# Order-only edges in the queues of ScalarE and VectorE, and a combination in two parts, in a decoder layer of split fp32r products

## The chip, the cores and the metric

The kernel runs on one core of a Trainium2 chip. The metric is the device time of one execution in microseconds (us). Times are compared as medians of several executions; the profile and the trace come from one further execution, whose own time stands beside its span.

## The reference, cut to what matters

One layer of a decoder over 256 tokens of width 2048, batch 1, in float32: a gated FFN half-step, a mixing stage (differential attention and an mLSTM scan from one input projection, one output projection), a second gated FFN half-step, and a last norm.

```python
x = x + 0.5 * swiglu(rmsnorm(x, ffn1_norm), ffn1_w_gate, ffn1_w_up, ffn1_w_down)   # D_FF = 5632
h = rmsnorm(x, mix_norm)
a_q, a_k, a_v, m_q, m_k, m_v, m_o, m_i, m_f = split(h @ w_in)
y_a = diff_attention(...)          # 4 heads, causal
y_b = mlstm(...) * sigmoid(m_o)    # 4 heads, causal
x = x + concat(y_a, y_b) @ w_out
x = x + 0.5 * swiglu(rmsnorm(x, ffn2_norm), ffn2_w_gate, ffn2_w_up, ffn2_w_down)
return rmsnorm(x, final_norm)
```

Nearly all of the work is products of a 256-row activation with weight matrices that are read once from HBM.

## The kernel before, in words

**Products in two halves.** Every operand of a large product is split in two fp32r parts: `hi`, a copy of it in fp32r on ScalarE (line 116), and `lo`, the rest, a subtraction on VectorE (line 117). For each pair of tiles `mms` (lines 142 to 149) issues three matmuls of 128x512: hi of the activation with hi of the weights (line 146), lo with hi (line 147), and, after all jobs of the call, hi with lo (line 149). So line 149 is the first to need a VectorE result (`wl`), line 146 the first to need ScalarE's (`wh`). Split weights live in `wsp`, four buffers of each half; a buffer comes free when the matmuls that read it are done.

**Pairs of outputs by seven products.** Two neighbouring chunks of 512 output columns are computed together by class `Paired` (lines 359 to 500), a Strassen-like scheme on the first `ns` blocks of the contraction (`ns` is 4 in the gate and up products, 2 in the first pair of them, 3 or 1 in the down products, 3 in the input projection, 2 in the output projection). `first` works on four PSUM banks p1, p6, p7, p5: for each block j, `load(j)` (line 381) fetches four 128x512 weight tiles into one `raw` buffer (pool `wr`, four buffers) by two DMAs on SyncE's queue, then VectorE forms two pair sums into `sums[j]` (line 388; the tile takes a slot of pool `wrp`, five slots, tag `rawp`, which the plain loads use too) and a third sum in place (line 390). `p57(j)` splits the sums and multiplies into p7 and p5; `p16(j)` splits two tiles of `raw`, multiplies into p1 and p6, and then has POOL issue a DMA that adds one tile of `raw` to another (line 409). For the last block p16 comes before p57. `combine` (lines 430 to 439) then joins the banks: ScalarE copies p1 to `u` (434), VectorE adds p6 to it (435) and it to p7 (436), ScalarE copies p7 to `u3` (437), VectorE subtracts (438, 439). `second` goes on in p1, p7 and p5 with the blocks' remaining tiles (`bare`, `upper`) and with `plain` units, ordinary products of the rest of the contraction, each loaded as one 512 KB `rawp` tile. `third` finishes the other output chunk and is left as a stream of units.

**The order of the work.** `Chain.run` (lines 511 to 527) writes the program order by hand: it steps through `first` of the next pair and lets units of the last pair's `third` run in between, then calls `combine`, then the end of the last pair (gate product, transposes, additions), then `second`. TensorE's own queue follows this order. The queues of the other engines are laid out by the framework's scheduler when the program is built, by priorities: loads, sums and splits are placed as if they stood 400 instructions earlier (`AHEAD`, with `high_priority`), and "seam" work, which is what stands between two pairs (the combination, the gate's SiLU at line 325, its product at line 329, the halved copy `part` at line 292), 440 earlier (`soon`). Each engine then runs its queue strictly in the order laid out. Semaphores between engines are made by the framework.

**The FFNs.** `ffn` (lines 535 to 584) runs 11 chunks of the hidden width in parts of 3, 3, 3 and 2; each part ends with two pairs of the down product. In the last part these pairs have one block (`ns == 1`) and three plain units. In the first FFN the first gate product is an ordinary one (`linear`, line 562), during which `load_xt` (line 591) loads and splits the transposed input; `sum_xt` (line 618) makes the sums of one activation block: two scalings on ScalarE (through line 344), three additions on VectorE (283 to 285) and a split. It is called once in `load_xt` and again at line 567, and two more times from the list `pending`.

## Time and profile before

| | |
|---|---|
| median of 3 runs | 1796.76 us (1793.56 to 1799.55) |
| the profiled execution | 1798.07 us |
| its span | 1796.4 us |
| granted TensorE clock, mean over the span | 0.997 |
| instructions | 23431 |
| read from HBM / written | 349.56 MB / 2.10 MB |

The span runs from the first to the last instruction of the program. In the timelines a row is: start in us from the span's start, duration in us, engine, line, operation, tile written and tiles read, shapes, number of instructions merged in the row, and in brackets the idle time of the engine before it with what ended it. PE is TensorE's matmuls, PEld its weight loads, DVE VectorE, ACT ScalarE, POOL GpSimd, SP SyncE.

### The profile page before, as it was taken

To read this page: it belongs to the slowest core of one execution; us is meant where nothing else is said; L and a number is where in the kernel's file an instruction comes from. 1 tells how busy PE (TensorE), PEld (TensorE's weight loads), DVE (VectorE), ACT (ScalarE), POOL (GpSimd) and SP (SyncE) were. 2 spreads that over 40 slices of the span, in tenths; PEclk is the share of its full clock that TensorE was granted. 3 is DMA by queue.
4 is the path that set the end of the run, shared out by engine and by line. 5 is a ranking of instruction groups with operands and counts; after the bars stand their busy time and mean duration, and the time that the engine had idled before them with its cause. 6 is when DMAs were issued, how large, how long until landed. Compare 5 with 4: busy or idle time off the path is not lost.

```text
span 1796.4 us, 23431 instructions
## 1 busy us (share of the span) xinstructions
PE 1773.1 (99%) x8033; PEld 1463.6 (81%) x8033; DVE 1566.1 (87%) x1895; ACT 1163.8 (65%) x1512; POOL 176.7 (10%) x220
## 2 busy tenths in 40 slices
PE   9999999999999999999999999999999999999998
PEld 6788888887888878987888888888888888888886
DVE  6988899988998877796787988999899988998886
ACT  6666666666666656676566766666666666666664
POOL 0001100111002100000000000001100111002100
PEclk9999999999999999999999999999999999999999
DMA  9777877887788863665656665778877788778864
GB/s 340 220 226 223 239 230 231 258 237 223 218 261 235 257 236 122 209 215 196 196 191 197 192 194 165 220 240 249 233 243 232 249 236 243 211 254 239 262 193 152
DMA packets 124649, 402.76 MB, mean 224 GB/s; under 512 B 14001, under 2 KB 14513, under 8 KB 124273
## 3 DMA queue, kind: packets, MB, share of 16 engines
q1 hardware_dynamic: 96192, 349.35, 56.6%
q0 software_dynamic: 27328, 49.82, 16.5%
q10 hardware_dynamic: 1008, 2.09, 0.3%
q8 instruction: 63, 1.03, 0.2%
q14 instruction: 58, 0.47, 0.1%
HBM read 349.56 MB, written 2.10 MB: 196 GB/s over the span
## 4 chain that ended last, share of the span: by engine, by line
PE 86%; DMA 5%; issue 4%; DVE 4%; ACT 1%; SPq 0%; POOL 0%; DVEq 0%; POOLq 0%; ACTq 0%
PE acc L146 28%; PE acc L149 27%; PE acc L147 27%; DVE wl L117 2%; DMA raw<-in_wu_dram 2%; DMA rawp<-in_wu_dram 2%; PE tr L307 1%; ACT wh L116 1%; DVE sums L388 1%; DMA raw<-raw 0%; PE tr L250 0%; PE sc L946 0%; SPq L173 0%; PE num L897 0%; PE tr L689 0%
## 5 line engine op out<-in xcount | busy, mean ns | idle before, releaser
L116 ACT CAST wh<-raw 128x1024 fp32r<-128x1024 f32 (+3 forms) x448 | 402.0, 906 | 282.6 <-PE acc L147 180.4
L146 PE MATMUL acc<-wh,xt 128*128 128x512 f32 (+3 forms) x1444 | 559.8, 389 | 3.1 <-ACT wh L116 3.0
L147 PE MATMUL acc<-wh,xt 128*128 128x512 f32 (+3 forms) x1444 | 557.0, 387 | 0.0
L117 DVE TENSOR_TENSOR wl<-raw,wh 128x1024 fp32r<-128x1024 f32 (+3 forms) x448 | 459.7, 1039 | 86.2 <-ACT wh L116 83.2
L116 ACT CAST wh<-rawp 128x1024 fp32r<-128x1024 f32 (+1 forms) x358 | 372.7, 1044 | 156.0 <-PE acc L147 133.3
L117 DVE TENSOR_TENSOR wl<-rawp,wh 128x1024 fp32r<-128x1024 f32 (+1 forms) x358 | 430.9, 1207 | 44.9 <-ACT wh L116 41.6
L146 PE MATMUL acc<-wh,xs 128*128 128x512 f32 (+2 forms) x1071 | 420.2, 393 | 6.7 <-ACT wh L116 2.9
L147 PE MATMUL acc<-wh,xs 128*128 128x512 f32 (+2 forms) x1071 | 414.8, 388 | 0.0
L149 PE MATMUL acc<-wl,xt 128*128 128x512 f32 (+3 forms) x1444 | 398.5, 386 | 0.4 <-DVE wl L117 0.4
L149 PE MATMUL acc<-wl,xs 128*128 128x512 f32 (+2 forms) x1071 | 335.9, 389 | 2.7 <-DVE wl L117 2.5
L146 PEld LDWEIGHTS acc<-wh,xt 128*128 128x128 f32 x1444 | 271.5, 188 | 60.6 <-ACT wh L116 5.8
L147 PEld LDWEIGHTS acc<-wh,xt 128*128 128x128 f32 x1444 | 271.6, 188 | 54.0
L149 PEld LDWEIGHTS acc<-wl,xt 128*128 128x128 f32 x1444 | 269.7, 188 | 54.7 <-DVE wl L117 0.8
L146 PEld LDWEIGHTS acc<-wh,xs 128*128 128x128 f32 x1071 | 201.5, 188 | 49.0 <-ACT wh L116 3.7
L149 PEld LDWEIGHTS acc<-wl,xs 128*128 128x128 f32 x1071 | 200.1, 188 | 47.3 <-DVE wl L117 6.9
L409 POOL DMA_DIRECT2D raw<-raw x141 | 121.5, 863 | 1187.8 <-DVE wl L117 852.4
L147 PEld LDWEIGHTS acc<-wh,xs 128*128 128x128 f32 x1071 | 201.5, 188 | 39.4 <-DVE xs L112 0.4
L388 DVE TENSOR_TENSOR sums<-raw 128x1024 f32<-128x1024 f32 x141 | 171.8, 1219 | 43.7 <-DMA raw<-in_wu_dram 38.9
L116 ACT CAST wh<-sums 128x1024 fp32r<-128x1024 f32 x141 | 148.5, 1053 | 83.7 <-PE acc L147 62.6
L117 DVE TENSOR_TENSOR wl<-sums,wh 128x1024 fp32r<-128x1024 f32 x141 | 171.8, 1219 | 12.5 <-ACT wh L116 10.1
L390 DVE TENSOR_TENSOR raw<-sums,raw 128x512 f32<-128x512 f32 x141 | 96.3, 683 | 0.8
L293 POOL DMA_DIRECT2D xres<-part x48 | 44.4, 1002 | 265.6 <-ACT part L292 264.4
(199 smaller groups left out, 804.4 us busy)
## 6 DMA issues: line engine op xcount, KB each, us to landing
rawp<-in_wd_dram SPq DMA_DIRECT2D x96, 512.0 KB, 5.6
rawp<-in_wu_dram SPq DMA_DIRECT2D x94, 512.0 KB, 7.5
raw<-in_wg_dram SPq DMA_DIRECT2D x89, 512.0 KB, 7.1
rawp<-in_wg_dram SPq DMA_DIRECT2D x86, 512.0 KB, 6.0
raw<-in_wu_dram SPq DMA_DIRECT2D x82, 512.0 KB, 7.8
raw<-in_wd_dram SPq DMA_DIRECT2D x80, 512.0 KB, 6.2
raw<-raw POOLq DMA_DIRECT2D x141, 256.0 KB, 6.2
rawp<-in_win_dram SPq DMA_DIRECT2D x50, 512.0 KB, 4.9
```

The source lines that it names most:

```text
L116: nc.scalar.copy(hi, src)
L117: nc.vector.tensor_tensor(out=lo, in0=src, in1=hi.bitcast(F32), op=ALU.subtract)
L146: nc.tensor.matmul(acc, lh, rh, start=first, stop=False, skip_group_check=on)
L147: nc.tensor.matmul(acc, ll, rh, start=False, stop=False, skip_group_check=on)
L149: nc.tensor.matmul(acc, lh, rl, start=False, stop=last, skip_group_check=on)
L293: nc.gpsimd.dma_start(xres[:, hb, c * CW:(c + 1) * CW], t, accum_op=ALU.add)
L307: nc.tensor.transpose(tr[:, i, hb * P:(hb + 1) * P], hs[hb][:, k * P:(k + 1) * P], ident)
L388: nc.vector.tensor_tensor(out=sums[j], in0=raw[:, 0:4:3, :], in1=raw[:, 2:3, :].to_broadcast([P, 2, CW]), op=ALU.add)
L390: nc.vector.tensor_tensor(out=raw[:, 2, :], in0=sums[j][:, 0, :], in1=raw[:, 3, :], op=ALU.add)
L409: nc.gpsimd.dma_start(raw[:, 2, :], raw[:, 1, :], accum_op=ALU.add)
```

## The change

It adds edges between two instructions of the same engine that fix their order in its queue and bring no semaphore (dependency class NoSync), and moves some steps in program order:

- Weight splits are counted (`splits`). A pair sum (line 388) may not stand ahead of the low half of the fourth split before it (`SUMS = 4`).
- Seam instructions are put in a list with the count at that time (`ahead_of_splits`); the split that is made four or more splits later (`SLACK = 4`) must stand behind them: its hi behind those of ScalarE, its lo behind those of VectorE. These are `part`, the gate's SiLU and product, and four of the six steps of the combination.
- The combination is cut in two: `combine` (copy of p1, addition of p6) is called right behind the last block's p16, `combine_rest` behind its p57, both inside `first`; before, all of it was called behind the units of the other stream.
- In pairs with one block, `second` puts the first plain unit ahead of `bare` and `upper`, and the hi split of `bare` must stand behind the second copy (`u3`).
- The second call of `sum_xt` moves from line 567, which stands behind four units of the first up product, into `load_xt`, where it now stands beside the first call at the last two units (6 and 7) of the first gate product.

```diff
@@ -43,6 +43,8 @@
 WARM = 10
 LAST_UNITS = 3
 CUTS = ((0, 544, 0), (1088, 1568, 1), (544, 1088, 0), (1568, 2048, 1))
+SLACK = 4
+SUMS = 4
 FLUSH = 3
 
 G_FFN1, G_MIX, G_FFN2, G_CW, G_CB, G_ATT, G_ML = 0, 16, 32, 48, 80, 88, 96
@@ -113,8 +115,29 @@
                                        op0=ALU.mult, op1=ALU.subtract)
 
     def split(src, hi, lo):
-        nc.scalar.copy(hi, src)
-        nc.vector.tensor_tensor(out=lo, in0=src, in1=hi.bitcast(F32), op=ALU.subtract)
+        return (nc.scalar.copy(hi, src),
+                nc.vector.tensor_tensor(out=lo, in0=src, in1=hi.bitcast(F32), op=ALU.subtract))
+
+
+
+    splits, queued = [], ([], [])
+
+    def after(late, early):
+
+        tc.add_manual_dep(late.ins, early.ins.name,
+                          mybir.DependencyInfo(mybir.DependencyClass.NoSync, mybir.DependencyReason.DATA),
+                          reason="order")
+
+    def ahead_of_splits(i, ins):
+        queued[i].append((len(splits), ins))
+
+    def split_weights(src, hi, lo):
+        made = split(src, hi, lo)
+        for late, q in zip(made, queued):
+            while q and len(splits) >= q[0][0] + SLACK:
+                after(late, q.pop(0)[1])
+        return made
+
 
     def pair_tiles(pool, tag, shape):
         return (pool.tile(shape, F32R, tag=tag + "h", name=nm(tag + "h")),
@@ -135,8 +158,9 @@
         with tc.high_priority(offset=AHEAD):
             o = 0
             for n in pieces:
-                split(raw[:, o:o + n, :], hi[:, o:o + n, :], lo[:, o:o + n, :])
+                made = split_weights(raw[:, o:o + n, :], hi[:, o:o + n, :], lo[:, o:o + n, :])
                 o += n
+        splits.append(made)
         return hi, lo
 
     def mms(jobs):
@@ -289,7 +313,7 @@
 
         t = wk("part")
         with soon():
-            nc.scalar.activation(t, acc, AF.Copy, scale=0.5)
+            ahead_of_splits(0, nc.scalar.activation(t, acc, AF.Copy, scale=0.5))
         nc.gpsimd.dma_start(xres[:, hb, c * CW:(c + 1) * CW], t, accum_op=ALU.add)
 
     def residual(accs, c, scale, parts):
@@ -322,11 +346,11 @@
     def gate(src, r):
         s = wk("sg")
         with soon():
-            nc.scalar.activation(s, src, AF.Silu, scale=r)
+            ahead_of_splits(0, nc.scalar.activation(s, src, AF.Silu, scale=r))
         return s
 
     def gated(src, r, s):
-        nc.vector.scalar_tensor_tensor(s, src, r, s, op0=ALU.mult, op1=ALU.mult)
+        ahead_of_splits(1, nc.vector.scalar_tensor_tensor(s, src, r, s, op0=ALU.mult, op1=ALU.mult))
         return s
 
     def soon(extra=40):
@@ -385,14 +409,16 @@
                     for i, w in enumerate((self.wa, self.wb)):
                         load_pair(raw[:, 2 * i:2 * i + 2, :], w, self.k0 + 2 * j)
                     sums[j] = wrp.tile([P, 2, CW], F32, tag="rawp", name=nm("sums"))
-                    nc.vector.tensor_tensor(out=sums[j], in0=raw[:, 0:4:3, :],
-                                            in1=raw[:, 2:3, :].to_broadcast([P, 2, CW]), op=ALU.add)
+                    made = nc.vector.tensor_tensor(out=sums[j], in0=raw[:, 0:4:3, :],
+                                                   in1=raw[:, 2:3, :].to_broadcast([P, 2, CW]), op=ALU.add)
+                    if len(splits) >= SUMS:
+                        after(made, splits[-SUMS][1])
                     nc.vector.tensor_tensor(out=raw[:, 2, :], in0=sums[j][:, 0, :], in1=raw[:, 3, :], op=ALU.add)
 
             def halves_of(src):
                 with tc.high_priority(offset=AHEAD):
                     t = pair_tiles(wsp, "w", [P, 2, CW])
-                    split(src, *t)
+                    splits.append(split_weights(src, *t))
                 return t
 
             def p57(j):
@@ -412,15 +438,20 @@
             p57(0)
             yield
             p16(0)
+            if last == 0:
+                self.combine()
             for j in range(1, self.ns):
                 load(j)
                 if j < last:
                     p57(j)
                 p16(j)
+                if j == last:
+                    self.combine()
                 if j % 2 and j < last - 1 or j == last:
                     yield
                 if j == last:
                     p57(j)
+            self.combine_rest()
             yield
 
         def steps(self):
@@ -428,13 +459,19 @@
             return {1: 2, 2: 3, 3: 3}.get(self.ns, 4)
 
         def combine(self):
-            u, u3 = wk("u"), wk("u3")
-            p1, p5, p6, p7 = self.p1, self.p5, self.p6, self.p7
+
+            self.u = wk("u")
             with soon():
-                nc.scalar.copy(u, p1)
-                nc.vector.tensor_tensor(out=u, in0=p6, in1=u, op=ALU.add)
-                nc.vector.tensor_tensor(out=p7, in0=p7, in1=u, op=ALU.add)
-                nc.scalar.copy(u3, p7)
+                ahead_of_splits(0, nc.scalar.copy(self.u, self.p1))
+                ahead_of_splits(1, nc.vector.tensor_tensor(out=self.u, in0=self.p6, in1=self.u, op=ALU.add))
+
+        def combine_rest(self):
+            u, u3 = self.u, wk("u3")
+            p5, p6, p7 = self.p5, self.p6, self.p7
+            with soon():
+                ahead_of_splits(1, nc.vector.tensor_tensor(out=p7, in0=p7, in1=u, op=ALU.add))
+                self.copied = nc.scalar.copy(u3, p7)
+                ahead_of_splits(0, self.copied)
                 nc.vector.tensor_tensor(out=p6, in0=p5, in1=u3, op=ALU.subtract)
                 nc.vector.tensor_tensor(out=p5, in0=p5, in1=u, op=ALU.subtract)
 
@@ -456,7 +493,9 @@
             def bare(j):
                 with tc.high_priority(offset=AHEAD):
                     t = pair_tiles(wsp, "w", [P, 2, CW])
-                    split(self.raws[j][:, 1:3, :], *t)
+                    splits.append(split_weights(self.raws[j][:, 1:3, :], *t))
+                    if self.ns == 1:
+                        after(splits[-1][0], self.copied)
                 mms([self.job(n11, j, A2, t, 0, False, False, True), self.job(n21, j, B2, t, 1, False, False, True)])
 
             def upper(j0):
@@ -464,20 +503,28 @@
                     t = pair_tiles(wsp, "w", [P, 2, CW])
                     js = range(j0, min(j0 + 2, self.ns))
                     for i, j in enumerate(js):
-                        split(self.raws[j][:, 3, :], t[0][:, i, :], t[1][:, i, :])
+                        made = split_weights(self.raws[j][:, 3, :], t[0][:, i, :], t[1][:, i, :])
+                splits.append(made)
                 mms([self.job(n12, j, S4, t, i, False, False, True) for i, j in enumerate(js)])
 
             for i in range(max(self.ns, len(self.rest))):
                 aside(side)
-                if i < self.ns:
-                    bare(i)
-                    if i % 2 or i == self.ns - 1:
-                        upper(i - i % 2)
+                def blocks():
+                    if i < self.ns:
+                        bare(i)
+                        if i % 2 or i == self.ns - 1:
+                            upper(i - i % 2)
+
+                if self.ns > 1:
+                    blocks()
                 if i < len(self.rest):
                     if i < len(self.rest) - 1:
                         self.plain(self.wa, self.rest[i], (n11, n21))
                     else:
                         self.plain(self.wa, self.rest[i], (n11, n21), True)()
+                if self.ns == 1:
+
+                    blocks()
                 flush(0 if i % 2 else None)
                 aside(mid)
             return [n11, n21]
@@ -521,7 +568,6 @@
                     done += 1
                 flush(1)
                 aside(side)
-            p.combine()
             self.end()
             half(p.second())
             self.put(p.third(last_units), len(p.rest), lambda: end(p.accs()))
@@ -564,7 +610,6 @@
                     stream = units(au, xp, wu[0], KD, fine=True)
                     for _ in range(KD // UK - NP):
                         next(stream)
-                    first[1]()
                     chain.put(stream, NP, functools.partial(end, au))
                 else:
                     np_ = NP
@@ -607,7 +652,7 @@
                 hi, lo = plain_pair(xp1, u)
             for t in range(UK):
                 split_gain(raw[:, t, :], G_FFN1 + k + t, hi[:, t, :], lo[:, t, :])
-        if u == KD // UK - 1:
+        if u >= KD // UK - NP_FIRST:
             sum_xt()
         if u >= KD // UK - NT:
```

## Rows read from the trace of the kernel before

**Rows 1.** The page, part 1: busy us of each engine, share of the span, instructions.
```profile
PE 1773.1 (99%) x8033; PEld 1463.6 (81%) x8033; DVE 1566.1 (87%) x1895; ACT 1163.8 (65%) x1512; POOL 176.7 (10%) x220
```

**Rows 2.** Busy time by stretch: length, engines, granted clock, DMA share, GB/s.
```profile
14.00:667.00 653.00, 647.95 (x2886) 533.77 (x2885) 578.03 (x647) 422.02 (x506) 71.61 (x82) 1.00 0.80 242
667.00:677.00 10.00, 6.98 (x23) 4.95 (x22) 9.27 (x12) 4.85 (x7) 0.00 (x0) 0.83 0.58 179
677.00:1786.00 1109.00, 1106.63 (x5099) 918.65 (x5098) 969.18 (x1213) 725.35 (x981) 101.68 (x123) 1.00 0.70 214
```

**Rows 3.** Waits of TensorE's matmuls: us in total, times, longest.
```profile
PE acc L146 <- ACT wh L116: 5.9, 7, 2.5
PE acc L149 <- DVE wl L117: 2.9, 7, 0.6
...
PE acc L146 <- ACT u L434: 0.4, 1, 0.4
```

**Rows 4.** Timeline of TensorE, 199 to 209 us.
```profile
200.19 0.39 PE L147 MATMUL acc<-wh,xs 128*128 128x512 f32 x1
201.17 0.73 PE L149 MATMUL acc<-wl,xs 128*128 128x512 f32 x2 [0.59 <-DVE wl L117]
...
208.10 0.61 PE L149 MATMUL acc<-wl,xs 128*128 128x512 f32 x2
```

**Rows 5.** Timeline of VectorE, 186 to 209 us.
```profile
190.74 1.23 DVE L388 TENSOR_TENSOR sums<-raw 128x1024 f32<-128x1024 f32 x1 [3.06 <-DMA raw<-in_wu_dram]
...
198.77 1.21 DVE L388 TENSOR_TENSOR sums<-raw 128x1024 f32<-128x1024 f32 x1
199.90 1.21 DVE L117 TENSOR_TENSOR wl<-raw,wh 128x1024 fp32r<-128x1024 f32 x1
...
206.37 1.23 DVE L117 TENSOR_TENSOR wl<-raw,wh 128x1024 fp32r<-128x1024 f32 x1 [1.24 <-ACT wh L116]
```

**Rows 6.** Timeline of VectorE, pieces from 82 to 1738 us.
```profile
82.63 2.35 DVE L388 TENSOR_TENSOR sums<-raw 128x1024 f32<-128x1024 f32 x2
...
140.84 1.23 DVE L388 TENSOR_TENSOR sums<-raw 128x1024 f32<-128x1024 f32 x1
...
152.30 1.22 DVE L117 TENSOR_TENSOR wl<-rawp,wh 128x1024 fp32r<-128x1024 f32 x1
...
161.68 1.22 DVE L117 TENSOR_TENSOR wl<-sums,wh 128x1024 fp32r<-128x1024 f32 x1
...
1736.90 1.22 DVE L388 TENSOR_TENSOR sums<-raw 128x1024 f32<-128x1024 f32 x1
```

**Rows 7.** Timeline of TensorE, 661 to 677 us.
```profile
661.58 0.62 PE L149 MATMUL acc<-wl,xs 128*128 128x512 f32 x2
...
667.70 0.39 PE L147 MATMUL acc<-wh,xs 128*128 128x512 f32 x1
669.93 0.50 PE L146 MATMUL acc<-wh,xs 128*128 128x512 f32 x1 [1.85 <-ACT u L437]
670.27 0.40 PE L147 MATMUL acc<-wh,xs 128*128 128x512 f32 x1
670.51 0.63 PE L149 MATMUL acc<-wl,xs 128*128 128x512 f32 x2
672.30 0.67 PE L146 MATMUL acc<-wh,xs 128*128 128x512 f32 x1 [1.17 <-DVE acc L439]
...
676.05 0.39 PE L146 MATMUL acc<-wh,xt 128*128 128x512 f32 x1
```

**Rows 8.** Timeline of ScalarE, 655 to 674 us.
```profile
665.01 1.57 ACT L116 CAST wh<-raw 128x1024 fp32r<-128x1024 f32 x2 [6.71 <-PE acc L149]
666.49 0.58 ACT L434 COPY u<-acc 128x512 f32<-128x512 f32 x1
```

**Rows 9.** One operation of the combination: duration ns min/median/max, first and last start.
```profile
L436 DVE TENSOR_TENSOR acc<-acc,u x44: 687/691/700, 56.8 to 1767.0; 128x512 f32<-128x512 f32 x44
```

**Rows 10.** Timeline of ScalarE, 33 to 46 us.
```profile
39.24 1.27 ACT L325 ACTIVATE sg<-acc,rstd 128x512 f32<-128x512 f32 x2 [1.95 <-POOL rstd L231]
40.40 1.70 ACT L344 ACTIVATE xg<-xraw,prm 128x256 f32<-128x256 f32 x4
```

## The prediction

> **What bounds the kernel now.** I read the busy shares first [rows 1]: TensorE's matmuls cover 1773.1 of 1796.4 us, so only time in which TensorE starts nothing can be won. Then the busy time by stretch [rows 2]: from 677 to 1786 us the weight loads are busy 918.65 of 1109 us (0.828) at granted clock 1.00; from 14 to 667 us 533.77 of 653 (0.817); from 667 to 677 us only 4.95 of 10, at clock 0.83. So the losses sit in the first FFN and above all in ten microseconds at its end. Then TensorE's waits [rows 3] for what ended them. Last the timelines around single waits, matmuls beside the two queues that feed them.
>
> One measure is needed throughout. A matmul record lasts 0.39 us, but the next one starts after 0.227 us: in [rows 4] the pair that starts at 208.10 lasts 0.61, so its second starts 0.22 after its first. An idle time in the list of waits is therefore short by 0.39 - 0.227 = 0.16 us: between 200.19 and 201.17 pass 0.98 us, 0.75 more than the pace, where the row says 0.59.
>
> The Trainium skill ("Perfetto Trace Analysis", Identifying the Most-Contended Engine) calls matmul occupancy a bad measure of headroom and the busy share of the weight loads a good one. By it, at 0.828 everywhere, re-ordering could give 653 - 533.77/0.828 = 8.4 us and 10 - 4.95/0.828 = 4.0 us, 12.4 in all; by matmul occupancy it would be 653 - 647.95 + 10 - 6.98 = 8.1. The waits below, counted from start to start, bear out the larger one.
>
> **Part 1, pair sums held back.** VectorE takes its queue in order. At 190.74 a pair sum heads it and waits 3.06 us for a load [rows 5]; the queue then runs without a gap until past 203. At 198.77 the sum of the pair's last block goes first and takes 1.13 us until the next start, and the low half that starts at 199.90 is the one TensorE waits for at 201.17 [rows 4, 5]. That sum belongs to the block whose low half starts at 206.37, four splits on. The new edge puts each sum behind the low half of the fourth split before it: here behind the one at 199.90, which then starts 1.13 us sooner. The wait costs 0.75, so it goes. I counted the same way, in the order of VectorE's queue: 80 of the 141 sums (the first at 82.63, the last at 1736.90 [rows 6]) stand ahead of the low half that they must now follow, and each wait of TensorE for a low half in the list has such a sum right in front of it. The list has 2.9 us in 7 waits [rows 3]; with 0.16 each, 2.9 + 7 x 0.163 = 4.0 us. All are shorter than 1.13 us.
>
> What is late next: at 206.37 + 1.23 = 207.60 a low half is ready whose matmul starts at 208.10 [rows 4, 5], so 0.50 of margin meets 0.75 regained, and 0.25 is lost again. I take 3.8 us, with 0 and 4.5 (two shorter waits that the list leaves out) as ends.
>
> What it costs: no instruction is added, each edge joins two instructions of one engine and asks for no semaphore (class NoSync). Twelve sums now run nine splits ahead: the one at 140.84 moves behind the low half at 152.30 [rows 6], 11.5 us later, still three splits before its own at 161.68. Its 1.13 us moves out of a stretch with margin into the next. It hides in the idle time before the sum at 190.74 (3.06 us) and its like. Without that cover it is 1.13 us on the low halves behind it. I take 0. The sum frees no slot of the loads (those of `raw` go with the last split of the block), so SyncE's queue is not held up by it; it takes its own `rawp` slot later, which frees that slot for a load. POOL's accumulating transfer follows the block's first split and stays behind it.
>
> **Part 2, the combination in two parts, and seam work ahead of later splits.** At 666 us is the pair with one block (`ns == 1`). Its last p1 product starts at 661.58 [rows 7], so the copy of p1 could run from about 662.2. ScalarE waits 6.71 us for a free split buffer, splits two tiles for work after the seam at 665.01, and only then, at 666.49, copies p1 [rows 8]. TensorE, after the matmul of 667.70, gets p7 at 669.93 and p5 at 672.30 [rows 7]. Lost: 669.93 - 667.70 - 0.227 = 2.0 us; from 669.93 to 672.30 four matmuls start, 2.37 - 4 x 0.227 = 1.46; after this gap the granted clock fell (0.83 over the ten microseconds [rows 2]) to the lower of its two levels, 1.2 GHz: from 672.30 to 676.05 nine matmuls took 3.75 instead of 2.04 us, 1.7 lost. Together 5.2 us. The same from counts: 23 matmuls in that stretch instead of 10/0.227 = 44 would be 4.8.
>
> In the changed kernel the copy is traced right after p16, ahead of the stream's units, and the block's next split gets an edge behind the second copy. By rows: copy 0.58 from 662.2 [rows 8], then two additions of 0.69 [rows 9] and a copy like the first, 2.5 us in all, done at 664.8, in time in which both engines are idle. TensorE comes there at 667.5. If a plain unit's split still goes ahead (665.01 to 666.0), the chain ends near 668.6, while the plain unit's first half covers until 667.47 + 4 x 0.227 = 668.4: 0.2 lost. I take 5.0, ends 2.0 (only the first wait goes, the clock still falls) and 5.2. Moving the blocks behind the first plain unit leaves the number of matmuls alone; the slot of `raw` comes free 12 matmuls, 2.7 us, later, and with it SyncE's next load into it, which lies beside matmuls. bare and upper issue no transfer; nothing on POOL moves.
>
> The second pair of this kind loses 0.4 + 0.16 = 0.6 us waiting for the p1 copy [rows 3]; the copy moves ahead of the last splits in front of it: 0.6, ends 0 and 0.6. The list of waits names a copy or an addition of the combination nowhere else, so in the other 42 pairs the earlier first half gives 0; were it to hold up splits, its price is 0.58 us of ScalarE per pair, beside TensorE. The same holds for the edges that put gates, half-scaled copies and products ahead of later splits: I counted them in the queues of before and none stands behind more than four splits, so they bind nothing now.
>
> **Part 3, the second sum_xt earlier.** Four scalings (1.70 us) lie on ScalarE at 40.40, right behind the gate that waited 1.95 us [rows 10]. Two are of the call that is moved. The two of the call that was already early stand in the same place behind the gate, so the nearest row says that nothing moves: 0. At best the list's waits for a high half shrink by what is not the kernel's start: (5.9 - 2.5) + 6 x 0.16 = 4.4 us [rows 3], which also holds the waits for late `rawp` loads; at worst 0.8 us of scalings stand before something urgent.
>
> **Sum.** 3.8 + 5.0 + 0.6 = 9.4 us. The profiled execution took 1798.07, so 1788.7 on its own time; the median shown, 1796.76, is 1.3 below, which gives **1787.4**. A measurement of this kernel can tell about 0.3%, 5.4 us, from no change.
>
> **Rivals.**
> - *Buffers, not order.* The waits for low halves come at the same place of many pairs. The Trainium skill ("Perfetto Trace Analysis", Optimization Strategy) reads the same bubble repeating as too little room for the next tile. As a mechanism here: the loss starts with the 3.06 us in which VectorE waits for a load whose slot came free late [rows 5], and the backlog stays whichever low half goes first; the wait moves on. For it: 0.50 us of margin just behind. Against: one swap of 1.13 exceeds each wait. Part 1 then gives 0: 1796.8 - 5.6 = 1791.2. The page's reading gives this time too. Chance 0.16, split over "faster" and "same".
> - *The scheduler leaves the seam as it is.* The new place in the trace is no edge for the first copy; if the one-block pair still copies late, only part 1 and little else remain: 1796.8 - 4 = 1793. For it: today the copy has the higher priority and yet stands behind two splits. Against: the edge of the block's split. Chance 0.18, no change.
> - *Sums too late, slower.* Loads and sums share five `rawp` slots. A sum that must wait for the fourth low half before it may find its slot taken by a load that went ahead; its split, the next one that TensorE needs, is then late. Place: the first block of each of the 44 pairs. Price: a wait like those of today, 4.0/7 = 0.57 us, in each: 25 us, against the 9.4, 1812. It decides once a sum ends less than a split's time before its split is due. Against it: three splits still lie between. Chance 0.14.
>
> **How the numbers follow.** The forecast has 0.52. Faster 0.52 + 0.08 = 0.60, same 0.18 + 0.08 = 0.26, slower 0.14. The range takes in the forecast's bounds: 4.5 + 5.2 + 0.6 + 4.4 = 14.7 gives 1782 at the bottom, and 1791 and 1793 of the first two rivals stand at the top. The runs of before lie up to 3 us from their median; of that I add 1 below, where every bound would have to meet, and 4 above: 1781 to 1797. What is left out is the slow rival and a little.
>
> **What would show it.** In the profile after: the waits for low halves at L149 nearly gone; no sum in VectorE's queue in front of the fourth low half before its own; between 660 and 680 us the p1 copy at about 662, granted clock 1.00, and 44 matmuls in ten microseconds. I am wrong if waits for sums appear ahead of the first product of the pairs, if the p1 copy is still behind splits, or if the 2.9 us come back under another name.

## The result, and the profile after

| | before | after |
|---|---|---|
| median | 1797.57 us (1793.56 to 1799.55, 6 runs) | 1785.94 us (1785.17 to 1787.22, 6 runs) |
| the profiled execution, and its span | 1798.07, 1796.4 us | 1786.73, 1785.0 us |

The ratio is 0.9937, 95% interval 0.9924 to 0.995: 11.6 us faster by the medians, where 9.4 had been predicted. Two more measurements of the changed kernel, on other occasions, gave 1785.78 (0.9937, 0.9925 to 0.9949) and 1786.09 us (0.9941, 0.9929 to 0.9954).

Busy shares of the changed kernel, from part 1 of its page; they stand against [rows 1].

```profile
PE 1768.9 (99%) x8033; PEld 1463.0 (82%) x8033; DVE 1566.2 (88%) x1895; ACT 1160.8 (65%) x1512; POOL 175.6 (10%) x220
```

The work is the same to the instruction on each of the five; only time in which TensorE started nothing, or ran at the lower clock, has gone. Where, the busy time by stretch tells (columns as in [rows 2]):

```profile
14.00:667.00 653.00, 651.61 (x2908) 538.49 (x2907) 583.45 (x652) 423.36 (x506) 70.65 (x82) 1.00 0.79 242
667.00:677.00 10.00, 9.99 (x48) 7.84 (x47) 9.32 (x11) 6.82 (x10) 0.86 (x1) 1.00 0.99 375
677.00:1786.00 1109.00, 1097.31 (x5059) 911.49 (x5057) 965.65 (x1216) 721.07 (x981) 101.46 (x123) 1.00 0.70 214
```

The ten microseconds that held 23 matmuls at clock 0.83 [rows 2] now hold 48 at 1.00, short transposes among them. (The last window reaches past the new end at 1785.0.) This is no longer the place of the one-block pair, which TensorE now reaches 5 us earlier and leaves 10 us earlier. Its own ten microseconds are these:

```profile
657.00:667.00 10.00, 10.00 (x46) 8.28 (x45) 8.64 (x12) 4.87 (x7) 0.00 (x0) 1.00 0.32 85
```

TensorE's waits, against [rows 3]:

```profile
PE acc L170 <- ACT xs L113: 2.7, 2, 2.2
PE acc L170 <- ACT wh L118: 2.7, 5, 0.9
```

The line for low halves (`wl`) and the one for `u` are gone; the line for high halves fell from 5.9 to 2.7. Of that fall 2.5 us is only a change of name: the long wait at the kernel's start stood in this line before and stands in the line for `xs` now. In the new numbering the high and low splits are lines 118 and 119, the three matmuls 170, 171 and 173, the pair sum 412, the third sum 416, the copies of p1 and p7 465 and 473, SyncE's loads 197.

Counted from start to start of matmuls, beyond the pace of 0.227 us (0.11 for transposes; the first 15 us from the last warm-up matmul on), the profiled executions differ so:

| place | lost before | lost after |
|---|---|---|
| waits for low halves, nine before, one after | 4.5 | 0.2 |
| first one-block pair, near 667 us | 5.2 | 0 |
| second one-block pair, near 697 us: `u` 0.59, residual transposes 0.65 | 1.2 | 0 |
| high halves near 45 and 50 us | 1.8 | 0 |
| high halves of late unit loads, five places | 2.8 | 3.55 |
| the first 15 us | 5.6 | 6.3 |

Together some 11 less, and the span is 11.4 shorter. The second row can be had in another way: the same 57 matmuls and transposes around that pair start within 17.13 us before (661.58 to 678.71) and within 11.93 after (656.71 to 668.64).

VectorE's queue, 183 to 205 us, the stretch of [rows 5]:

```profile
195.51 1.22 DVE L119 TENSOR_TENSOR wl<-raw,wh 128x1024 fp32r<-128x1024 f32 x1
...
198.38 1.22 DVE L119 TENSOR_TENSOR wl<-sums,wh 128x1024 fp32r<-128x1024 f32 x1
199.52 1.22 DVE L412 TENSOR_TENSOR sums<-raw 128x1024 f32<-128x1024 f32 x1
200.65 1.22 DVE L119 TENSOR_TENSOR wl<-raw,wh 128x1024 fp32r<-128x1024 f32 x1
...
203.72 1.23 DVE L119 TENSOR_TENSOR wl<-raw,wh 128x1024 fp32r<-128x1024 f32 x1 [1.24 <-ACT wh L118]
```

The urgent low half, which ran at 199.90 right behind the pair's last sum [rows 5], is here the one at 195.51. The sum, at 199.52, now stands behind it, and TensorE takes that low half at 198.64 without a wait. ScalarE's queue at the one-block pair, 650 to 668 us, against [rows 8]:

```profile
657.14 0.59 ACT L465 COPY u<-acc 128x512 f32<-128x512 f32 x1 [0.98 <-PE acc L173]
659.22 0.59 ACT L473 COPY u<-acc 128x512 f32<-128x512 f32 x1 [1.49 <-DVE acc L472]
660.37 1.57 ACT L118 CAST wh<-raw 128x1024 fp32r<-128x1024 f32 x2 [0.57 <-DMA raw<-raw]
```

Both copies run ahead of the two splits (`bare` and `upper`) that stood before the first of them.

### The profile page after: what moved, and what is told of

Read it like the earlier page. It is cut to its first block, busy times and chain, and to the rows that moved or that the text cites. A ratio compares the mean times of both kernels' runs of the same rounds, so it can differ in the third digit from the quotient of the medians.

```text
span 1785.0 us, 23399 instructions
## 1 busy us (share of the span) xinstructions
PE 1768.9 (99%) x8033; PEld 1463.0 (82%) x8033; DVE 1566.2 (88%) x1895; ACT 1160.8 (65%) x1512; POOL 175.6 (10%) x220
## 4 chain that ended last, share of the span: by engine, by line
PE 95%; DMA 2%; ACT 1%; issue 0%; DVE 0%; SPq 0%; POOLq 0%; POOL 0%; ACTq 0%; DVEq 0%
PE acc L170 31%; PE acc L173 31%; PE acc L171 31%; DMA rawp<-in_wu_dram 2%; PE tr L331 1%; ACT wh L118 1%; PE tr L274 0%; PE sc L991 0%; PE num L942 0%; DMA raw<-in_wg_dram 0%; DVE wl L119 0%; SPq L197 0%; PE tr L734 0%; PE tr L1030 0%; PE rr L912 0%
```

## The experiments

Each ran beside the kernel before on the same chip; ratios are to that kernel. The changed kernel itself ran beside experiments four and six and the later half of seven; its medians on three chips lie within 0.3 us of each other. Unless a diff is named as one against the kernel before, it is against the changed kernel.

**One: no edges on the sums.**

```diff
-SUMS = 4
+SUMS = 1 << 30
```

> The changed kernel without the edges on the pair sums (part 1 undone, the rest kept). If the edges themselves end the waits for low halves, these come back at the first products of the last blocks: about 2.9 us of idle time in some 7 waits, 4 us from start to start, so about 1790 us against 1785.9. If it was another part of the change that moved them (the queue is laid out anew each time), or if room in the buffers sets them, the time stays within 1 us of 1785.9 and the list of waits names no low half.

Measured: 1787.4 us (1787.04 to 1787.7), ratio 0.9951 (0.9939 to 0.9964). TensorE's waits of that run have the line again:

```profile
PE acc L173 <- DVE wl L119: 1.7, 3, 0.7
```

From start to start the low halves cost 2.9 us in six places, 2.7 more than with the edges. The time rises by 1.5 us by the medians; the changed kernel was not run beside it, and by the ratios it is 2.5.

**Two: the kernel before, with the sums' edges alone** (the diff is against the kernel before: line 388 and its edge as in the change, all else as it was).

```diff
+                    made = nc.vector.tensor_tensor(out=sums[j], in0=raw[:, 0:4:3, :],
+                                                   in1=raw[:, 2:3, :].to_broadcast([P, 2, CW]), op=ALU.add)
+                    if len(splits) >= SUMS:
+                        after(made, splits[-SUMS][1])
```

> The kernel before with part 1 alone: the edges on the pair sums; combination, blocks and sum_xt as they were, no edges for the seam. If the edges on the sums end the waits for low halves by themselves, the time is 2.7 to 4 us below before, and these waits are gone while those at the one-block pair stay. If part 1 needs the earlier seam work, the gain is under 1.5 us and waits for low halves stay in the list.

Measured: 1794.91 us (1792.0 to 1799.42, 12 runs), ratio 0.9989 (0.9981 to 0.9998), some 2 us: less than the 2.7 to 4 expected, though the waits named are gone. TensorE's waits:

```profile
PE acc L170 <- ACT wh L118: 6.7, 9, 1.5
PE acc L170 <- ACT u L473: 3.0, 1, 3.0
PE acc L170 <- DVE acc L476: 1.4, 2, 0.9
```

No wait for a low half is left, without any new buffer and without the rest of the change. But other lines grew: the high halves from 5.9 to 6.7, and the first wait at the one-block pair to 3.0 where it was 1.85 [rows 7]. TensorE came sooner to places that did not become ready as much sooner. The waits for late unit loads are 3.7 us from start to start, 2.8 before.

**Three: the old order of blocks in one-block pairs.** `bare` and `upper` again ahead of the first plain unit, and no edge of `bare` behind `u3`.

```diff
-                    if self.ns == 1:
-                        after(splits[-1][0], self.copied)
...
-                if self.ns > 1:
-                    blocks()
+                blocks()
...
-                if self.ns == 1:
-                    blocks()
```

> In pairs with one block, bare and upper stand ahead of the first plain unit again, and the hi split of bare has no edge behind the second copy; the combination stays in two parts. If the order of the blocks and that edge are what keeps the copy of p1 ahead of the splits, TensorE waits again at the one-block pair of the first FFN: 2 us for p7 and more for p5, with the granted clock down for some us behind it, 2 to 5 us in all (1788 to 1791). If the early first half of the combination does it, nothing returns: 1786.

Measured: 1791.79 us (1789.45 to 1795.33, 11 runs), ratio 0.9978 (0.9969 to 0.9987), so 5.9 us of the gain are lost by the medians (7.4 by the ratios). TensorE's waits, then ScalarE's queue and the window of that run:

```profile
PE acc L170 <- ACT u L473: 3.5, 2, 3.1
```

```profile
661.69 1.57 ACT L118 CAST wh<-raw 128x1024 fp32r<-128x1024 f32 x2 [7.19 <-DMA raw<-raw]
663.17 0.58 ACT L465 COPY u<-acc 128x512 f32<-128x512 f32 x1
666.99 0.58 ACT L473 COPY u<-acc 128x512 f32<-128x512 f32 x1 [3.24 <-DVE acc L472]
```

```profile
667.00:677.00 10.00, 9.37 (x37) 7.23 (x38) 9.94 (x12) 6.82 (x9) 0.00 (x0) 0.83 0.66 221
```

The copy of p1 stands early in program order and is still laid out behind the two splits, and these wait 7.19 us for the accumulating transfer that POOL issues. The combination comes late, TensorE idles 3.1 us, and the clock falls as before. So at this pair it is the order of the blocks with its edge that saves the time; the new place of the first half does not do it alone. Which of the two, order or edge, was not run apart. How the program is laid out tells part of it. With the edge and the old order of the blocks, both copies stand ahead of the two splits in ScalarE's queue, as in the changed kernel; with the new order and no edge, the split of `bare`, the one that reads what the transfer writes, still stands ahead of the copy of p1. So it is the edge that brings the copies forward; what the new order adds in time is not shown.

**Four: the combination in one piece at its old place**, with the blocks' order and edge kept.

```diff
@@ Paired.first
-            if last == 0:
-                self.combine()
...
-                if j == last:
-                    self.combine()
...
-            self.combine_rest()
@@ Chain.run
-            self.end()
+            p.combine(); p.combine_rest(); self.end()
```

> The whole combination again behind the units of the other stream, as before the change; the order of the blocks, the edge behind the second copy and all other edges stay. If the order of the blocks with that edge is what keeps the copy of p1 early, the one-block pair of the first FFN shows no wait and at most 0.6 us return at the second such pair: 1786 to 1786.6. If the early first half is needed, the waits for p7 and p5 return there with the lower clock: 1788 to 1791.

The changed kernel ran once more beside it:

> The changed kernel once more, beside the others of this set on one chip: 1785 to 1787 us. It is the yardstick for differences of one or two microseconds.

Measured: 1788.8 us (1787.96 to 1789.34), ratio 0.9951 (0.9938 to 0.9964); the changed kernel 1785.78 (1785.01 to 1787.53), so 3.0 us. TensorE's waits:

```profile
PE acc L170 <- ACT u L473: 0.9, 1, 0.9
PE acc L170 <- ACT u L465: 0.4, 1, 0.4
PE tr L274 <- DVE xres L322: 0.2, 1, 0.2
```

None of these is at the first one-block pair: all lie between 687 and 692 us, at the second (0.59 and 1.07 from start to start, and 0.8 on the transposes before). The early first half is worth 3 us, 2.5 of it there; another 0.4 is a wait for a high half at 50.11 us.

**Five: sum_xt at its old place.**

```diff
-        if u >= KD // UK - NP_FIRST:
+        if u == KD // UK - 1:
...
+                    first[1]()
```

> The second sum_xt back behind four units of the first up product. If its two scalings on ScalarE and three additions on VectorE were what made the high halves late at about 45 and 50 us, both waits return, 1.2 and 0.6 us from start to start, and the first 15 us give back some 0.5 us that the early call costs there: 1 to 1.8 us, 1787 to 1787.7. If those waits went for another reason (edges elsewhere), the time stays at 1786 and no wait stands between 40 and 55 us.

Measured: 1786.35 us (1785.6 to 1789.01), ratio 0.9951 (0.9938 to 0.9965), against 1785.94 in its own comparison and 1785.8 to 1786.1 in three: 0.4 us, no more than these scatter. (By the ratios it is 2.5 us, with intervals that overlap: this run alone decides little.) In the trace two waits return, of 0.67 and 1.14 from start to start, the first of them for a low half this time:

```profile
45.85 1.20 PE L173 MATMUL acc<-wl,xt 128*128 128x512 f32 x4 [0.51 <-DVE wl L119]
49.39 0.50 PE L170 MATMUL acc<-wh,xs 128*128 128x512 f32 x1 [0.98 <-ACT wh L118]
```

The first 15 us lose 4.0 in place of 4.2 to 6.3. What happens at the seam is in ScalarE's queue of the changed kernel, 33 to 48 us:

```profile
38.83 1.27 ACT L349 ACTIVATE sg<-acc,rstd 128x512 f32<-128x512 f32 x2 [1.04 <-POOL rstd L255]
39.98 0.90 ACT L368 ACTIVATE xg<-xraw,prm 128x256 f32<-128x256 f32 x2
40.78 1.04 ACT L118 CAST wh<-sums 128x1024 fp32r<-128x1024 f32 x1
```

Two scalings stand behind the gate, where there were four [rows 10]. The other two have moved to the start:

```profile
4.26 0.91 ACT L368 ACTIVATE xg<-xraw,prm 128x256 f32<-128x256 f32 x2 [1.51 <-DMA prm<-in_par_dram]
...
7.22 0.89 ACT L368 ACTIVATE xg<-xraw,prm 128x256 f32<-128x256 f32 x2
```

The row at 7.22 is the moved call. The call that was early already has its scalings at 4.26, and it had them at 4.20 in the kernel before, whose queue shows this at the start, and this behind the four scalings of [rows 10]:

```profile
4.20 0.91 ACT L344 ACTIVATE xg<-xraw,prm 128x256 f32<-128x256 f32 x2 [1.45 <-DMA prm<-in_par_dram]
...
42.00 1.04 ACT L116 CAST wh<-sums 128x1024 fp32r<-128x1024 f32 x1
```

**Six: sums one and two low halves later.**

```diff
-SUMS = 4
+SUMS = 2
```

> A pair sum may stand no further ahead than the second split before it instead of the fourth. If sums that come late are the danger (the slow rival of the prediction), the first products of the pairs now wait for their sums' split, 0.5 us or more in most of the 44 pairs: 1800 us or more. If one split's time of TensorE still covers a sum (1.13 us) and its split (1.05 us), only the places where VectorE is behind anyway lose: below 3 us, up to 1789.

Measured: 1851.72 us (1849.89 to 1855.16), ratio 1.0305 (1.0291 to 1.0318), on the side of the first theory and far above its 1800, but mostly at another place than the split of the sums. TensorE's waits, then VectorE's, ScalarE's and TensorE's queue around one of them:

```profile
PE acc L170 <- ACT wh L118: 32.7, 27, 2.3
```

```profile
296.43 1.22 DVE L119 TENSOR_TENSOR wl<-raw,wh 128x1024 fp32r<-128x1024 f32 x1
297.56 1.22 DVE L412 TENSOR_TENSOR sums<-raw 128x1024 f32<-128x1024 f32 x1
298.81 0.69 DVE L416 TENSOR_TENSOR raw<-sums,raw 128x512 f32<-128x512 f32 x1
```

```profile
299.66 1.04 ACT L118 CAST wh<-raw 128x1024 fp32r<-128x1024 f32 x1 [3.46 <-issue]
```

```profile
300.75 0.50 PE L170 MATMUL acc<-wh,xs 128*128 128x512 f32 x1 [2.08 <-ACT wh L118]
```

A chain: low half, pair sum, third sum, high half of the tile that the third sum writes, matmul, each starting when the one before it is done or nearly so. (The row of the split names no releaser, only "issue"; that it waits for the third sum is read from the times.) Of the 27 waits 17, with 21.1 of the 32.7 us, are of this kind: the split of a `raw` tile starts within 0.15 us of the end of a third sum, and in six of them the trace names that sum as the releaser. Eight are for splits of plain units (9.3 us) and two for splits of sums (2.3). The sum shown does not wait for a slot (there is no idle time before 297.56); it is late by its place alone. The rest of the 66 us lies in many short losses and in matmuls at a slower pace behind the gaps: the mean granted clock is 0.989 where the changed kernel has 0.997.

Then the value between:

```diff
-SUMS = 4
+SUMS = 3
```

> The changed kernel with SUMS = 3 in place of 4: each pair of sums goes behind a split one low half later. With 2 the rival's mechanism (sums, third sum, high half of the product unit, matmul) ended 27 waits of 32.7 us and the time rose by 66 us; with 4 none is in the list. Theory A (the margin at 4 is about one low half, and a step of one takes half of what two take, so the edge of the slow side lies between 2 and 3): at 3 few or none of these waits, 1784 to 1790 us. Theory B (the slow side begins right below 4): a good part of the waits is there already, 10 to 20 of over 1 us, 1805 us or more.

Measured: 1785.33 us (1784.3 to 1787.18), ratio 0.994 (0.9927 to 0.9953): the changed kernel's time (1786.09 on the same chip). No line for low halves, and for high halves this:

```profile
PE acc L170 <- ACT wh L118: 2.2, 4, 0.9
```

So one low half of margin is free, and the next one costs 66 us.

**Seven: the changed kernel again, and the late unit loads.** The waits that grew with the change end with a plain unit's load. SyncE's queue of the changed kernel, 444 to 466 us, and ScalarE's and TensorE's behind it:

```profile
445.88 0.51 SPq L197 DMA_DIRECT2D raw<-in_wu_dram  x1
454.42 0.33 SPq L197 DMA_DIRECT2D raw<-in_wg_dram  x1
454.80 0.42 SPq L197 DMA_DIRECT2D raw<-in_wu_dram  x1
455.27 1.02 SPq L197 DMA_DIRECT2D rawp<-in_wu_dram  x2
```

```profile
462.63 1.05 ACT L118 CAST wh<-rawp 128x1024 fp32r<-128x1024 f32 x1 [1.32 <-DMA rawp<-in_wu_dram]
```

```profile
463.73 0.50 PE L170 MATMUL acc<-wh,xt 128*128 128x512 f32 x1 [0.42 <-ACT wh L118]
```

The unit's loads are issued from 455.27 on, right behind two loads of a block that waited until 454.42 for their `raw` buffer. The theory: these two hold it up, in the same way as the sums held up the low halves, and an order-only edge in SyncE's queue cures it. In this version the loads of a block (from the third block of a pair on) stand behind the loads of plain units that were traced before them.

```diff
 def load_pair(raw, w, k):
-        nc.sync.dma_start(dst, w[k // LK][:, k % LK:k % LK + 2, :])
+        return nc.sync.dma_start(dst, w[k // LK][:, k % LK:k % LK + 2, :])
...
-            load_pair(raw, w, k)
+            unit_loads.append(load_pair(raw, w, k))
...
-                        load_pair(raw[:, 2 * i:2 * i + 2, :], w, self.k0 + 2 * j)
+                        m = load_pair(raw[:, 2 * i:2 * i + 2, :], w, self.k0 + 2 * j)
+                        if unit_loads and j >= 2:
+                            after(m, unit_loads[-1])
```

> One edge more, in SyncE's queue: the load of a block from the third on (j of 2 or more) stands behind the loads of all plain units that come before it in program order. Five waits of 0.5 to 1.0 us for a high half (274, 463, 1160, 1348 and 1535 us in the changed kernel, 3.5 us from start to start) stand behind a load of a plain unit that was issued behind a load of a block waiting for its buffer. If that order is their cause, they go: up to 3.5 us, 1782.5. If the load is late because the transfers themselves share the DMA engines (some 7 us to landing), they stay: 1786.

Measured: **1780.73 us** (1780.44 to 1781.48), ratio 0.9915 (0.9901 to 0.9929). Once more, beside the changed kernel on one chip:

> The changed kernel with the edge in SyncE's queue, once more, now beside the changed kernel on the same chip. If what it gave is the removal of the five late loads of plain units (3.5 us in the changed kernel's trace, and the clock and spread of the start besides), 1780 to 1782.5 us, 3.5 to 5.5 us under the changed kernel, and no high-half wait behind such a load. If it was a lucky run, within 2 us of the changed kernel.

> The changed kernel as it is, beside the run with the edge in SyncE's queue on the same chip. 1785 to 1787 us; high-half waits behind the late loads of plain units of 2.5 to 4 us in sum.

Measured: 1780.72 us (1780.23 to 1780.92), ratio 0.9912 (0.9898 to 0.9925), against 1786.09 (1784.85 to 1787.09) for the changed kernel: 5.4 us less, with ranges that do not meet. SyncE's queue of this second run, and TensorE's one wait for a high half:

```profile
444.84 0.55 SPq L197 DMA_DIRECT2D raw<-in_wu_dram  x1
445.44 4.29 SPq L197 DMA_DIRECT2D rawp<-in_wu_dram  x2
453.18 0.33 SPq L197 DMA_DIRECT2D raw<-in_wg_dram  x1
```

```profile
PE acc L170 <- ACT wh L118: 0.3, 1, 0.3
```

The two unit loads leave within 4.29 us from 445.44, ahead of the block loads at 453.18. From start to start the late high halves between 200 and 2000 us cost 4.5 us in the changed kernel's trace of this comparison (3.7 and 4.3 in the two earlier ones) and 0.4 here. That is 4.1 of the 5.4 us. The start does not give the rest, since it loses 1.2 us more here than in that trace of the changed kernel (5.4 against 4.2); the rest lies in losses of less than 0.15 us each, whose cause is not shown.

And this version with sum_xt at its old place, as in experiment five:

> The edge in SyncE's queue, and the second call of sum_xt at its old place. If the new place is worth what the single run of the old place showed (0.4 to 0.6 us: two waits of 1.8 us return, but the start is shorter), 1781 to 1782 us. If the start's part of that was chance, 1782 to 1783 us; if the new place gives nothing, 1780 to 1781 us.

Measured: 1781.35 us (1781.03 to 1782.73), ratio 0.9917 (0.9905 to 0.9929), 0.6 more than with the new place; the ranges do not meet, though barely, and the range of this version's first measurement, on another chip, reaches past it (1781.48). The waits near 46 and 49 us are back (1.8 in sum), and the start loses 3.7 where it lost 5.4.

## Why the prediction was right, and which of its steps were not

The forecast (1787.4, faster) held, and the time came out 1.5 us below it. Undone one by one, the parts are worth 5.9 (blocks), 3.0 (early first half), 1.5 (sums) and 0.4 to 0.6 (sum_xt) by the medians, 11 us in sum, against 11.6. This agreement is looser than it looks: by the ratios the blocks are worth 7.4 and the sums 2.5. The nearness of the forecast is in part luck as well. Part 1 was put 1.3 to 2.3 us too high, the second one-block pair 2.4 too low and sum_xt some 0.5 too low, and these errors cancel in part.

**Part 1, 3.8 us: the mechanism right, the size not.** The count of waits was good: 4.5 us of waits for low halves went to 0.2, and the edges alone clear that line. But a wait removed is not time gained in full. The edges are worth some 2 us on the kernel before and 1.5 to 2.5 on the changed one. On the kernel before, the waits for late unit loads and at the one-block pair grow when the edges come in: what ends those does not come as much sooner. "What is late next" was looked for at the next low half (the 0.25 near 206 us, which did not come), not in SyncE's queue, where it was.

**Part 2, 5.0 us at the first one-block pair: right.** 5.2 us went, and undoing the order of the blocks and its edge brings 5.9 back. One detail was misread. "ScalarE waits 6.71 us for a free split buffer" rested on the releaser named in [rows 8]; in experiment three the same two splits wait 7.19 us for the accumulating transfer. In the kernel before, that transfer was issued here and took 8.6 us, so it landed at some 664.9, and the splits started at 665.01:

```profile
656.27 0.86 POOL L409 DMA_DIRECT2D raw<-raw  x1 [30.33 <-DMA rawp<-in_wd_dram]
```

The matmul that the row names and the transfer ended together. The split needs the transfer in any case: in the changed kernel it waits for it too (0.57 us, at 660.37), but with both copies already done.

**Part 2, 0.6 us at the second pair: mis-sized.** It measured 3.0. The prediction priced only the wait for `u` that the list showed. The transposes ahead of it waited too (0.65), and without the early half the second copy is late as well (1.07 in experiment four), which in the kernel before did not show. That the earlier half gives nothing in the other pairs held: no other wait for a copy appears in experiment four. Without the SLACK edges the program is laid out with every engine's instructions in the same order, so, as predicted, those edges bind nothing; that variant was not run.

**Part 3, 0 us: the failed step.** The reason given, that the scalings of the call that was already early "stand in the same place behind the gate", was false, and a row that was not read shows it: in the kernel before that call's scalings ran at 4.20 us. The four at 40.40 were the moved call and a later one. With two gone, the split behind them came 1.2 us sooner (40.78 after 42.00; 0.4 of that because the gate itself came sooner), and both waits behind it (1.23 and 0.60) ended. That the time gained only about 0.5 us may be because the start pays: 3.7 to 5.6 us are lost in the first 15 with the old place (four traces), 4.2 to 6.3 with the new one (ten). But these ranges overlap, and the start differs between executions of one program, so this is not shown.

**The rivals.** *Buffers, not order* falls: edges alone cleared the waits, with the buffers as they were. That waits move on is nevertheless about half true, as Part 1 tells; whether more buffers would have done the same was not run. The bubble that repeats was here one of order, in VectorE's queue and again in SyncE's. The Trainium skill ("Perfetto Trace Analysis", Optimization Strategy) says of such a bubble that it can mean too little room for the next tile; these runs show a second cause. Of the two measures of headroom set out in the prediction, the weight loads' share was the better: some 10 us of the gain (3.0 at low halves, 5.2 and 1.8) lie in the two stretches from 14 to 677 us, where it allowed 12.4 and matmul occupancy only 8.1. *The scheduler leaves the seam as it is* is half true: experiment three shows the first copy at its new place in the trace and still behind two splits. The edge and the order of the blocks are what the rival left out. *Sums too late* did not happen at 4, and not at 3; at 2 it does, through the third sum and not through a taken slot, and at 66 us it is far dearer than the 25 of the rival.

## What to carry to other kernels

When a wait repeats, look at what stands in front of the awaited instruction in its in-order queue before adding buffers: an edge without a semaphore cost no instruction here, and the same look at the DMA queue gave another 5.4 us. A wait removed is worth its length only if what ends the next wait moves with it; here about half of what the sums' edges removed from the kernel before came back at other waits, the late loads among them, until their queue was put in order too. Hold work back by a margin found by trying both neighbours: three and four low halves were equal, two cost 66 us.

## What the runs showed of the hardware that was not expected

The start is not the same from one execution to the next. In two traces of the changed kernel, TensorE's queue from 0 to 16 us shows this behind the warm-up matmuls; first the profiled execution of the result, then the third measurement:

```profile
7.37 0.73 PE L170 MATMUL acc<-wh,xs 128*128 128x512 f32 x2 [2.16 <-ACT xs L113]
8.08 1.22 PE L171 MATMUL acc<-wh,xs 128*128 128x512 f32 x2
```

```profile
6.13 0.73 PE L170 MATMUL acc<-wh,xs 128*128 128x512 f32 x2 [0.95 <-ACT xs L113]
6.84 0.73 PE L171 MATMUL acc<-wh,xs 128*128 128x512 f32 x2
9.36 0.73 PE L170 MATMUL acc<-wh,xs 128*128 128x512 f32 x2 [1.78 <-ACT xs L113]
```

In the first, the second pair of matmuls behind a stop of 2.16 us takes 1.22 us: the granted clock is 0.50, the lower of its two levels (1.2 GHz), from 8 to 14.5 us. In the second, pairs take 0.73 behind stops of 0.95 and 1.78, at 1.00 over the same stretch. The trace between these two measurements has two stops, of 1.66 and 1.48, and the clock falls there too (0.51). The first 15 us lose 6.3, 4.2 and, in that one, 6.3 us, with the same program. That is as much as the smaller parts of this change are worth, so they had to be judged by where waits lie and not by a single time. What decides between the two was not tried.
